# FFN up projection: 18 of 22 column pairs as seven products of half matrices, with the weights' sums formed by transfers

## The chip, the cores and the metric

The kernel runs on one core of a Trainium2 chip. The metric is the device time of one execution in microseconds, as the median of several executions. One core has TensorE (PE) for matrix products, VectorE (DVE), ScalarE (ACT) and GpSimd (POOL) for element-wise work, SyncE (SP) for issuing transfers, and 16 DMA engines that move data between DRAM and the on-chip memory SBUF. Matrix products land in PSUM, which has eight banks.

## The reference

One inference layer of a decoder (width 1024) is applied to 512 prompt tokens and 64 sample tokens, 576 in all. A mixer of three branches (gated linear attention, pooling, windowed attention) is followed by a gated feed-forward network (FFN) with a causal convolution of width 3; a norm of the result follows. The change lies in the FFN's first half:

```
def conv_ffn(xn, conv_prev, w_up, conv_w, conv_b, w_down):
    a, b = jnp.split(xn @ w_up, 2, axis=-1)          # xn: 576 x 1024, w_up: 1024 x 5632
    ext = jnp.concatenate([conv_prev.astype(a.dtype), a], axis=1)
    y = conv_b + conv_w[0] * ext[:, 0:t_len] + conv_w[1] * ext[:, 1:t_len + 1] + conv_w[2] * ext[:, 2:t_len + 2]
    h = jax.nn.silu(y) * b
    return h @ w_down, ext[:, -(CONV_WIDTH - 1):]    # w_down: 2816 x 1024
```

All data are float32. The output also holds the updated caches: 48 copies of cache rows, 120 to 2040 KB each, go from DRAM to DRAM.

## The kernel before

Every float32 product is made of three faster ones. Each operand is cut into hi, a rounded copy in the type F32R, and lo, the rest; the product is hi x hi + hi x lo + lo x hi, summed in PSUM. The activations lie with features on partitions, as eight tiles of 128 x 576 (`xh2`, `xl2` for the FFN). The weights come as a stream of chunks of 1024 rows x 128 columns (512 KB), in their order of use:

- `Chunk.load` (line 152) has SP issue the transfer into the tile `wr`, which has 3 buffers.
- `Chunk.split` cuts the whole chunk at once: ACT casts it into `wh` (line 161, 128x1024) and DVE subtracts for `wl` (line 164), 2 buffers each. For the first two chunks of the kernel POOL subtracts.
- `fetch(i)` cuts chunks i and i+1 and loads i+2 and i+3.
- `products` (matmul at line 207) runs over a chunk's eight k and the three terms; `gemm` does so for two parts of the tokens, each in one of the three PSUM banks `g`, and hands the bank to an evacuation.

The FFN's up projection is a loop over f = 0 to 21. A round takes a column pair: 128 columns of a and the 128 of b that they gate. So a round has 2 x 2 x 8 x 3 = 96 matmuls. The norm's factor per token, `rst`, is applied when the banks are read.

```
1164   for part, before in zip(SPLIT, (None, total)):
           gemm(P["a", f], XH2, XL2, evac, (part,))       # parts of 256 and 320 tokens; evac: DVE, lines 1159 and 1161
       ...                                                # two POOL copies into cc (1170, 1171), side_copy
1184   V.tensor_scalar(y, ae[:, 0:592], fvec[:, f, 16:17], fvec[:, f, 19:20], op0=OP.mult, op1=OP.add)
1185   V.scalar_tensor_tensor(y, ae[:, 1:593], fvec[:, f, 17:18], y, op0=OP.mult, op1=OP.add)
1186   V.scalar_tensor_tensor(y, ae[:, 2:594], fvec[:, f, 18:19], y, op0=OP.mult, op1=OP.add)
1187   S.activation(y, y, AF.Silu)
1189   G.tensor_tensor(yr[:, :NP], y[:, :NP], rst[:, :NP], op=OP.mult)     # and 1190 for the samples
       gemm(P["b", f], XH2, XL2, times(yr))               # DVE multiplies out of PSUM, line 226
1194   S.copy(h_hi[f], yr)
1195   V.tensor_tensor(h_lo[f], yr, h_hi[f].bitcast(F32), op=OP.subtract)
```

(Some calls above are shortened; the numbers at the left are the profile's lines.) `ae` holds a with the convolution's two earlier tokens, for the prompt and each of eight samples. `side_copy` (line 183) issues one of the DRAM copies on POOL's queue; there is one in each round.

The down projection (matmul at line 1249) follows: for each of eight blocks of 128 output columns, 22 k x 3 terms x 2 token halves, all of the block at once. `rows_out` turns a finished block to token rows. Block 7 is done in two token parts, so that the end is short.

The order of the work on each engine comes from a planner that knows the dependencies, the buffers and modelled durations of the instructions; `tc.issue_after` adds single constraints. Each engine runs its list in that order.

Of the kernel before, what the change touches and what calls it, by code (L numbers as in the profile page):

```python
# [22 lines left out]
NF = FF // 128  # L23
EPS = 1e-6
# [78 lines left out]
def hybrid_step(ctx: ExitStack, tc: tile.TileContext, I, O, at_a, at_b):  # L103
# [6 lines left out]
    xpool = ctx.enter_context(tc.tile_pool(name="x", bufs=1, side="left"))  # L110
# [25 lines left out]
    # ------------------------------------------------------- weight stream  # L136
    WSLOT = 1024
    chunks = []

    class Chunk:  # L140
        def __init__(self, src, kt, cols):
            self.src, self.kt, self.cols = src, kt, cols
            self.loaded = self.cut = False

        def load(self):
            if self.loaded:
                return
            self.loaded = True
            self.raw = wpool.tile([128, WSLOT], F32, tag="wr", name="wr", bufs=3)
            n = self.kt * self.cols  # L150
            self.v = self.raw[:, :n].rearrange("p (k c) -> p k c", k=self.kt)
            self.dma = nc.sync.dma_start(self.v, self.src)

        def split(self):
            if self.cut:
                return
            self.cut = True
            self.load()
            n = self.kt * self.cols
            hi = wpool.tile([128, WSLOT], F32R, tag="wh", name="wh", bufs=2)  # L160
            S.copy(hi[:, :n], self.raw[:, :n])  # L161
            lo = wpool.tile([128, WSLOT], F32R, tag="wl", name="wl", bufs=2)
            E = G if self in chunks[:2] else V
            self.cut_at = E.tensor_tensor(lo[:, :n], self.raw[:, :n], hi[:, :n].bitcast(F32), op=OP.subtract)  # L164
            self.hi = hi[:, :n].rearrange("p (k c) -> p k c", k=self.kt)
            self.lo = lo[:, :n].rearrange("p (k c) -> p k c", k=self.kt)
# [11 lines left out]
    def side_copy(after):  # L178
        """one of the copies within DRAM, issued behind an instruction of the Pool engine"""
        if copies:  # L180
            dst, src = copies.pop(0)
            with tc.issue_after(after.ins):
                nc.gpsimd.dma_start(dst, src)
# [5 lines left out]
    def plan(name, c0, cols=128, r0=0, kt=8):  # L189
        chunks.append(Chunk(rows(name, c0, cols, r0, kt), kt, cols))  # L190
        return len(chunks) - 1

    def fetch(i):
        for n in range(i, min(i + 2, len(chunks))):
            chunks[n].split()
        for n in range(i + 2, min(i + 4, len(chunks))):
            chunks[n].load()

    def products(ps, ids, xh, xl, t0, t1, c=0):
        """weights' hi and lo against the activations' hi and lo, into ps [128, t1 - t0]"""  # L200
        ks = [(i, k) for i in ids for k in range(chunks[i].kt)]
        for n, (i, k) in enumerate(ks):
            if k == 0:
                fetch(i)
            w = chunks[i]
            for j, (a, b) in enumerate(((w.hi, xh), (w.hi, xl), (w.lo, xh))):
                T.matmul(ps[:, :t1 - t0], a[:, k, c:c + 128], b(n)[:, t0:t1],  # L207
                         start=(n == 0 and j == 0), stop=(n == len(ks) - 1 and j == 2))
# [19 lines left out]
    def power(r, ms, e):  # L228
        """r = (ms + e) ** -0.5, two small tiles of one shape"""
# [3 lines left out]
    # ------------------------------------------------------------ constants  # L233
# [14 lines left out]
    # ------------------------------------------------------------ the plan of weight chunks, in order of use  # L248
# [45 lines left out]
    for f in range(NF):  # L294
        P["a", f] = [plan("ffn_w_up", 128 * f)]
        P["b", f] = [plan("ffn_w_up", FF + 128 * f)]
    for m in (*range(8), 7):
# [1000 lines left out]
```

## Time and profile before

| | |
|---|---|
| median of 3 runs | 1327.64 us (1325.46 to 1327.8) |
| span of the profiled execution, first to last instruction | 1324.9 us |
| PE busy | 1305.0 us, 99% |
| DVE busy | 601.6 us, 45% |
| ACT busy | 464.3 us, 35% |
| POOL busy | 242.4 us, 18% |
| mean rate of the DMA engines | 141 GB/s |
| up projection | 887.5 to 1171.3 us of the span |

The profiled execution has no time of its own other than the span; the runs' median lies 2.7 us above it. A busy time is the union of an engine's instructions; the matmuls' ends are modelled, so their number and pitch say more than their single durations. The DMA share is the time that packets took, as a share of 16 engines, and can pass 1 where packets overlap.

### The profile page before, as it was taken

Reading aid. Unit: us, or ns where it says so; the run is one execution under the profiler, and the core shown is the slowest. Engines: PE = TensorE matmul, PEld = TensorE weight load, DVE = VectorE, ACT = ScalarE, POOL = GpSimd, SP = SyncE. Lnnn points to the kernel's source line nnn. Section 1 sums busy time; section 2 is a strip of 40 time slices with the busy share of each in tenths; the row PEclk is TensorE's granted clock in tenths of the full one; section 3 lists DMA queues with packets and bytes.
Section 4 is the critical chain, followed back from the end, with each engine's and each line's share of the span. In section 5 each row is a group of like instructions: output and inputs, shape, how many; then the busy total and the mean of one; then the engine's idle time right before and its main releaser. Section 6 shows DMA issues by size and latency. Waiting matters only on the chain.

```text
span 1324.9 us, 23686 instructions
## 1 busy us (share of the span) xinstructions
PE 1305.0 (99%) x9903; PEld 1257.5 (95%) x9903; DVE 601.6 (45%) x1004; ACT 464.3 (35%) x899; POOL 242.4 (18%) x398
## 2 busy tenths in 40 slices
PE   8899999999999999999999999999999999999997
PEld 6899999999999999998988889999999999999997
DVE  5754564433453333162633366435555555532223
ACT  6554553534321222242433343433222222222223
POOL 4320211022410112041311110122121212200000
PEclk9999999999999999999999999999999999999999
DMA  7232432355443557266676415363455555444333
GB/s 218 65 116 68 144 115 69 96 178 158 131 141 95 163 159 220 73 184 190 182 217 204 154 31 167 100 225 118 145 164 162 162 167 157 148 129 149 91 88 116
DMA packets 220582, 187.44 MB, mean 141 GB/s; under 512 B 7900, under 2 KB 216393, under 8 KB 219700
## 3 DMA queue, kind: packets, MB, share of 16 engines
q1 hardware_dynamic: 218682, 142.28, 36.8%
q0 software_dynamic: 1792, 43.65, 9.6%
q8 instruction: 78, 1.28, 0.4%
q14 instruction: 28, 0.23, 0.1%
q10 hardware_dynamic: 2, 0.00, 0.0%
HBM read 175.52 MB, written 54.27 MB: 173 GB/s over the span
## 4 chain that ended last, share of the span: by engine, by line
PE 94%; DVE 2%; ACT 2%; issue 1%; DMA 1%; POOL 0%; SPq 0%; POOLq 0%; DVEq 0%; ACTq 0%
PE g L207 63%; PE g L1249 8%; PE g L395 8%; PE h L1249 2%; PE h L936 1%; PE s L805 1%; PE s L207 1%; PE s L864 1%; PE s L828 1%; PE s L820 1%; PE s L881 1%; PE h L869 1%; PE s L611 0%; DVE bb L475 0%; PE s L591 0%
## 5 line engine op out<-in xcount | busy, mean ns | idle before, releaser
L207 PE MATMUL g<-xl,wh 128*128 128x288 f32 (+2 forms) x1664 | 494.1, 297 | 0.0
L207 PE MATMUL g<-xh,wh 128*128 128x288 f32 (+2 forms) x1664 | 494.1, 297 | 0.0
L207 PE MATMUL g<-xh,wl 128*128 128x288 f32 (+2 forms) x1664 | 492.8, 297 | 1.1 <-DVE wl L164 1.1
L161 ACT CAST wh<-wr 128x1024 fp32r<-128x1024 f32 (+3 forms) x181 | 184.4, 1019 | 485.8 <-PE g L207 287.8
L164 DVE TENSOR_TENSOR wl<-wr,wh 128x1024 fp32r<-128x1024 f32 (+3 forms) x179 | 227.1, 1268 | 252.9 <-ACT wh L161 252.2
L207 PEld LDWEIGHTS g<-xh,wl 128*128 128x128 f32 x1664 | 313.7, 189 | 3.3 <-issue 1.4
L207 PEld LDWEIGHTS g<-xl,wh 128*128 128x128 f32 x1664 | 314.1, 189 | 2.3 <-issue 2.0
L207 PEld LDWEIGHTS g<-xh,wh 128*128 128x128 f32 x1664 | 314.2, 189 | 1.1 <-issue 0.7
L395 PE MATMUL g<-wh,xh 128*128 128x256 f32 x224 | 72.1, 323 | 2.5 <-DVE vs L400 2.5
L1249 PE MATMUL g<-hh,wl 128*128 128x288 f32 (+2 forms) x286 | 72.2, 297 | 0.0
L1249 PE MATMUL g<-hh,wh 128*128 128x288 f32 (+2 forms) x286 | 72.0, 297 | 0.0
L395 PE MATMUL g<-wl,xh 128*128 128x256 f32 x224 | 71.5, 319 | 0.0
L1249 PE MATMUL g<-hl,wh 128*128 128x288 f32 (+2 forms) x286 | 71.5, 295 | 0.0
L395 PE MATMUL g<-wh,xl 128*128 128x256 f32 x224 | 71.4, 320 | 0.0
L395 PEld LDWEIGHTS g<-wh,xh 128*128 128x128 f32 x224 | 52.3, 233 | 5.7 <-DVE vs L400 2.7
L395 PEld LDWEIGHTS g<-wl,xh 128*128 128x128 f32 x224 | 52.3, 234 | 0.7 <-issue 0.7
L395 PEld LDWEIGHTS g<-wh,xl 128*128 128x128 f32 x224 | 52.4, 234 | 0.0
L1249 PEld LDWEIGHTS g<-hh,wl 128*128 128x128 f32 x286 | 49.8, 189 | 0.0
L1249 PEld LDWEIGHTS g<-hh,wh 128*128 128x128 f32 x286 | 49.6, 189 | 0.0
L1249 PEld LDWEIGHTS g<-hl,wh 128*128 128x128 f32 x286 | 49.6, 189 | 0.0
L1159 DVE TENSOR_TENSOR ae<-g,rst 128x256 f32<-128x256 f32 x44 | 18.6, 425 | 64.0 <-PE g L207 64.0
L226 DVE TENSOR_TENSOR yr<-yr,g 128x288 f32<-128x288 f32 x44 | 18.1, 451 | 49.8 <-POOL yr L1189 49.8
(453 smaller groups left out, 2179.9 us busy)
## 6 DMA issues: line engine op xcount, KB each, us to landing
wr<-in_w_in_dram SPq DMA_DIRECT2D x74, 512.0 KB
wr<-in_ffn_w_up_dram SPq DMA_DIRECT2D x44, 512.0 KB
out_dram<-in_cache_k_w_dram POOLq DMA_DIRECT2D x8, 2040.0 KB, 8.4
out_dram<-in_cache_v_w_dram POOLq DMA_DIRECT2D x8, 2040.0 KB, 8.3
kv<-in_cache_k_w_dram SPq DMA_DIRECT2D x26, 512.0 KB
kv<-in_cache_v_w_dram SPq DMA_DIRECT2D x26, 512.0 KB
wr<-in_ffn_w_down_dram SPq DMA_DIRECT2D x18, 448.0 KB
wr<-in_ffn_w_down_dram SPq DMA_DIRECT2D x9, 512.0 KB
```

Source lines behind the costliest of these rows:

```text
L161: S.copy(hi[:, :n], self.raw[:, :n])
L164: self.cut_at = E.tensor_tensor(lo[:, :n], self.raw[:, :n], hi[:, :n].bitcast(F32), op=OP.subtract)
L207: T.matmul(ps[:, :t1 - t0], a[:, k, c:c + 128], b(n)[:, t0:t1], start=(n == 0 and j == 0), stop=(n == len(ks) - 1 and j == 2))
L226: return lambda ps, t0, t1: V.tensor_tensor(t[:, t0:t1], t[:, t0:t1], ps, op=OP.mult)
L395: mm = T.matmul(dst, a, b[:, n % 4, :], start=(n == 0 and j == 0), stop=(n == 7 and j == len(seq) - 1))
L805: T.matmul(sp[:, nk * n:nk * n + nk], qT[r, p, 128 * t:128 * t + 128], kT[r, p, k0:k0 + nk], start=True, stop=True)
L820: T.transpose(pt[:, 128 * n:128 * n + 128], s4[:, h, 128 * kb:128 * kb + 128], ident)
L828: T.matmul(po[64 * hh:64 * hh + 64, 128 * x:128 * x + 128], vt[:, blocks[kb], 64 * (2 * p + hh):64 * (2 * p + hh) + 64], pts[:, (2 * x + h ...
L864: T.transpose(pk[:, 128 * n:128 * n + 128], kt[:, 2 * half + n // 2, 128 * (n % 2):128 * (n % 2) + 128], ident)
L869: T.matmul(sp[32 * b:32 * b + 32, 0:128], qz[:, p, 32 * b:32 * b + 32], kT[:, n, p, :], start=(r == 0 and p == 0), stop=(r == NR[g] - 1 an ...
L1159: V.tensor_tensor(ae[:, 2 + t0:258 + t0], ps[:, :256], rst[:, t0:t0 + 256], op=OP.mult)
L1249: T.matmul(q[:, :t1 - t0], a[:, k, :], b[n][:, t0:t1], start=(n == 0 and j == 0), stop=(n == NF - 1 and j == 2))
```

## The change

**Seven products.** For f from 4 to 21 a pair is computed as a 2 x 2 block product. The activations are halved by features (k 0 to 3 and 4 to 7) and by tokens (two of 288); the weights of a pair are halved by rows (upper and lower 512) and by a or b. The Winograd form of Strassen's scheme makes the four result blocks from seven products of half matrices instead of eight. A product has 4 k x 3 terms = 12 matmuls of 288 columns. The rounds f = 0 to 3 stay as they were (`NF0 = 4`).

**x's parts.** `sums_x(k)`, called once after each of the first four rounds, forms the normed activations of k and k+4, four sums of their halves, and hi and lo of the seven parts: on DVE 13 operations, on ACT seven copies.

**Weights' sums.** The four summed operands t3, t2, t1, t4 are formed in place: a transfer with accumulation, issued by POOL, adds half a chunk (256 KB, in rows of 512 B) from DRAM to the half chunk in SBUF. t3, t2 and t4 are successive values of the same half of b's chunk. A part is cut (ACT and DVE, 512 columns) between its accumulation and the next. Loads, accumulations and cuts stand at set steps before the unit's first product (a step is a product).

**Sums of products.** Products 0, 2, 4, 6 accumulate in one bank A, 3 and 5 in B, 1 in C. Between two products of a bank ACT copies the bank's content (`s1`, `u2`, `s5`), or DVE adds it.

**The rest.** The cuts of all weights are made in pieces of 512 columns with 4 buffers instead of 1024 with 2. In the FFN's up projection the side copies are issued by ACT behind the SiLU instead of by POOL; the convolution's first step moves from DVE to ACT; h is kept in float32 and cut after the last pair, for all 22 f, in a pool that opens where x's parts were (every fourth lo on POOL, the others on DVE). Blocks m = 0 and 1 of the down projection run together, by thirds of the k and halves of a third. Comments were removed.

```diff
+        def piece(self, p):
+            if p not in self.parts:
+                self.load()
+                n = self.kt * self.cols
+                E = G if self in chunks[:2] else V
+                hi, lo, self.cut_at = cut_part(self.raw[:, PART * p:min(PART * p + PART, n)], E)
+                self.parts[p] = hi, lo
...
+    X_OF = ("11", "21", "t2", "t1", "t3", "22", "t4")
+    x_parts = {n: [sx.tile([128, 4, HALF], F32R, name=f"x{part}_{n}") for part in ("h", "l")] for n in X_OF}
+    def sums_x(k):
+        top = fp.tile([128, NT], F32, tag="xn", name="xn", bufs=1)
+        bottom = fp.tile([128, 592], F32, tag="y", name="xn2", bufs=1)[:, :NT]
+        for t, m in ((top, k), (bottom, k + 4)):
+            V.scalar_tensor_tensor(t, x1[:, m, :], vecs[:, m, 1:2], rst, op0=OP.mult, op1=OP.mult)
+        a11, a21, a12, a22 = top[:, :HALF], top[:, HALF:], bottom[:, :HALF], bottom[:, HALF:]
+        s3, s1, s2 = (fp.tile([128, HALF], F32, tag=t, name=t, bufs=2) for t in "uvu")
+        V.tensor_tensor(s3, a11, a21, op=OP.subtract)
+        V.tensor_tensor(s1, a22, a21, op=OP.subtract)
+        V.scalar_tensor_tensor(s2, s1, -1.0, a11, op0=OP.mult, op1=OP.subtract)
+        V.scalar_tensor_tensor(a21, a12, -1.0, s2, op0=OP.mult, op1=OP.subtract)
+        for n, x in (("11", a11), ("21", a12), ("t4", a22), ("t3", s3), ("t1", s1), ("t2", s2), ("22", a21)):
+            hi, lo = x_parts[n]
+            S.copy(hi[:, k], x)
+            V.tensor_tensor(lo[:, k], x, f32(hi[:, k]), op=OP.subtract)
+    class Unit:
+        def load(self):
+            self.b.load()
+            self.a.load(sx, "wr2", 2)
+        def place(self, n):
+            c, h = {"11": (self.a, 0), "t1": (self.a, 0), "21": (self.a, 4), "22": (self.b, 4)}.get(n, (self.b, 0))
+            return c.v[:, h:h + 4, :]
+        def add(self, n):
+            c, h = {"t3": (self.b, 4), "t2": (self.a, 0), "t4": (self.a, 4), "t1": (self.b, 0)}[n]
+            nc.gpsimd.dma_start(self.place(n), c.src[:, h:h + 4, :], accum_op=OP.add)
+        def cut(self, n):
+            pool, tag, bufs = {"t3": (sx, "3", 2), "t4": (sx, "4", 1)}.get(n, (wpool, "", 4))
+            src = self.place(n).rearrange("p k c -> p (k c)")
+            hi, lo = (pool.tile([128, PART], F32R, tag=f"w{t}{tag}", name=f"w{t}", bufs=bufs) for t in "hl")
+            S.copy(hi, src)
+            V.tensor_tensor(lo, src, f32(hi), op=OP.subtract)
+    ORDER = ("11", "21", "t2", "t1", "t3", "22", "t4")
+    STEPS_W = {-12: [("load", None)], -11: [("add", "t3")], -5: [("cut", "t3"), ("add", "t2")], -4: [("cut", "11"), ("add", "t1")],
+               -2: [("cut", "21")], -1: [("cut", "t2"), ("add", "t4")], 0: [("cut", "t1")], 1: [("cut", "22")], 4: [("cut", "t4")]}
...
+    for f in range(NF0, NF):
+        s1, u2, s5 = part("u"), part("v"), part("s5", 1)
+        A, B, C = big()[:, :HALF], small()[:, :HALF], small()[:, :HALF]
+        product(u, 0, A, True, False)
+        S.copy(s1, A)
+        product(u, 1, C, True, True)
+        V.tensor_tensor(ae[:, 2:2 + HALF], s1, C, op=OP.add)
+        product(u, 2, A, False, False)
+        S.copy(u2, A)
+        product(u, 3, B, True, False)
+        S.copy(s5, B)
+        product(u, 4, A, False, False)
+        V.tensor_tensor(h[:, HALF:], A, s5, op=OP.add)
+        product(u, 5, B, False, True)
+        V.tensor_tensor(h[:, :HALF], B, u2, op=OP.add)
+        product(u, 6, A, False, True)
+        n = NP - HALF
+        S.copy(ae[:, 2 + HALF:2 + NP], A[:, :n])
+        S.copy(aes[:, :, 2:10], by_sample(A[:, n:]))
+        keep_state(f, ae, aes)
+        y = conv(f, ae)
+        side_copy(y_at, nc.scalar)
+        V.scalar_tensor_tensor(h[:, :NP], h[:, :NP], -1.0, y[:, :NP], op0=OP.mult, op1=OP.mult)
+        V.scalar_tensor_tensor(by_sample(h[:, NP:]), by_sample(h[:, NP:]), -1.0, by_sample(y[:, 512:592])[:, :, 2:10],
+                               op0=OP.mult, op1=OP.mult)
...
+    for f in range(NF):
+        S.copy(h_hi[f], hs[f])
+        (G if f % 4 == 3 else V).tensor_tensor(h_lo[f], hs[f], f32(h_hi[f]), op=OP.subtract)
...
+    turns = [(m, chunks[P["dn", m][t]], p) for t in range(3) for p in range(2) for m in range(2)]
...
+    for x, (m, c, p) in enumerate(turns):
+        pieces(x)
...
+        for k in range(4 * p, min(4 * p + 4, c.kt)):
+            down_rows(c, k, n[m], ps[m], EVEN)
```

More of the change, by code (lines that the diff above doesn't have):

```diff
@@ L134, in close_pool, with cut_part, __init__, load @@
         cm.__exit__(None, None, None)
+    x_cm, xpool = open_pool("x", "left")
     WSLOT = 1024
+    PART = 512
     chunks = []
+    def cut_part(src, E):
+        n = src.shape[1]
+        hi = wpool.tile([128, PART], F32R, tag="wh", name="wh", bufs=4)
+        S.copy(hi[:, :n], src)
+        lo = wpool.tile([128, PART], F32R, tag="wl", name="wl", bufs=4)
+        return hi, lo, E.tensor_tensor(lo[:, :n], src, hi[:, :n].bitcast(F32), op=OP.subtract)
     class Chunk:
[L141 to L145, printed above, removed]
+        def __init__(self, src, kt, cols, plain=True):
+            self.src, self.kt, self.cols, self.plain = src, kt, cols, plain
+            self.loaded, self.parts = False, {}
+        def load(self, pool=None, tag="wr", bufs=3):
             if self.loaded:
@@ L152, in load, with at, wide @@
             self.dma = nc.sync.dma_start(self.v, self.src)
-        def split(self):
[L155 to L166, printed above, removed]
+        def piece(self, p):
[5 more added lines that the diff above has]
+                self.parts[p] = hi, lo
+            return self.parts[p]
+        def split(self):
+            if self.plain:
+                for p in range((self.kt * self.cols + PART - 1) // PART):
+                    self.piece(p)
+        def at(self, k, c=0):
+            a = k * self.cols + c
+            return [t[:, a % PART:a % PART + 128] for t in self.parts[a // PART]]
+        def wide(self, k):
+            a = k * self.cols
+            return [t[:, a % PART:a % PART + self.cols] for t in self.parts[a // PART]]
     KEYS = (("cache_k_w128", "cache_v_w128"), ("cache_k_w512", "cache_v_w512"), ("cache_k_w2048", "cache_v_w2048"))
@@ new lines, in hybrid_step, with pieces @@
+    units = [Unit(f) for f in range(NF0, NF)]
+    ORDER = ("11", "21", "t2", "t1", "t3", "22", "t4")
+    STEPS_W = {-12: [("load", None)], -11: [("add", "t3")], -5: [("cut", "t3"), ("add", "t2")], -4: [("cut", "11"), ("add", "t1")],
+               -2: [("cut", "21")], -1: [("cut", "t2"), ("add", "t4")], 0: [("cut", "t1")], 1: [("cut", "22")], 4: [("cut", "t4")]}
+    turns = [(m, chunks[P["dn", m][t]], p) for t in range(3) for p in range(2) for m in range(2)]
+    def pieces(n):
+        for _, c, p in turns[n:n + 4]:
+            c.piece(p)
+        for _, c, _ in turns[n + 4:n + 8]:
+            c.load()
@@ new lines, in steps, with product @@
+    def steps(g):
+        for at in sorted(STEPS_W, reverse=True):
+            u, r = divmod(g - at, 7)
+            if r == 0 and 0 <= u < len(units):
+                for what, n in STEPS_W[at]:
+                    getattr(units[u], what)(*([n] if n else []))
+        if g >= 7 * len(units) - 3:
+            pieces(0)
+    def product(u, p, ps, start, stop):
+        steps(7 * u + p)
+        n = ORDER[p]
+        (wh, wl), (xh, xl) = units[u].parts[n], x_parts[n]
+        for k in range(4):
+            for j, (a, b) in enumerate(((wh, xh), (wh, xl), (wl, xh))):
+                T.matmul(ps, a[:, 128 * k:128 * k + 128], b[:, k, :], start=start and k == 0 and j == 0,
+                         stop=k == 3 and j == 2, skip_group_check=True)
@@ L1156, in hybrid_step, with keep_state @@
         G.tensor_copy(aes[:, :, 0:2], fvec[:, f, 0:16].rearrange("p (b n) -> p b n", b=8))
-        def evac(ps, t0, t1):
-            V.tensor_tensor(ae[:, 2 + t0:258 + t0], ps[:, :256], rst[:, t0:t0 + 256], op=OP.mult)
-            if t0:
-                V.tensor_tensor(aes[:, :, 2:10], ps[:, 256:].rearrange("p (b n) -> p b n", b=8),
-                                rst[:, NP:].rearrange("p (b n) -> p b n", b=8), op=OP.mult)
-        for part, before in zip(SPLIT, (None, total)):
-            with tc.issue_after(before.ins) if f == 0 and before else nullcontext():
-                gemm(P["a", f], XH2, XL2, evac, (part,))
+        return ae, aes
+    def keep_state(f, ae, aes):
+        nonlocal cc
         i = f % 7
```

166 lines of the change are left out of this document (114 added, 52 removed).

## The prediction

> **What bounds the kernel now.** I read the page's totals first, then the chain that ended last in order of time, then the stretch of the FFN's up projection by itself.
>
> ```profile
> span 1324.9 us, 23686 instructions
> ...
> PE 1305.0 (99%) x9903; PEld 1257.5 (95%) x9903; DVE 601.6 (45%) x1004; ACT 464.3 (35%) x899; POOL 242.4 (18%) x398
> ...
> PE 94%; DVE 2%; ACT 2%; issue 1%; DMA 1%; POOL 0%; SPq 0%; POOLq 0%; DVEq 0%; ACTq 0%
> ```
> ```profile
> 896.87 80.03 PE g L207 x603
> 977.00 89.22 PE g L207 x672
> 1066.34 89.22 PE g L207 x672
> 1155.67 12.74 PE g L207 x96
> 1168.52 2.80 PE g L207 x21
> 1171.32 17.69 PE g L1249 x133
> ```
> ```profile
> 887.50:1171.30 283.80, 283.80 (x2144) 283.76 (x2145) 153.29 (x243) 77.48 (x97) 59.62 (x152) 1.00 0.51 154
> ```
>
> The first fence says that TensorE is busy nearly throughout and is 94% of the chain. The second says that the up projection is one unbroken run of matmuls at line 207: 672 of them take 89.22 us, so one costs 132.8 ns, a column pair (96) 12.745 us, and the next stage (line 1249) follows at once. The third is the same stretch as a window (time, PE, weight loads, DVE, ACT, POOL, clock, DMA share, GB/s): PE 283.80 of 283.80 at clock 1.00, DVE 54%, ACT 27%, DMA 0.51. So the number of matmuls sets the end here, and a matmul fewer is worth 0.1328 us, as long as nothing else becomes the bound.
>
> **The change part by part.** *Matmuls.* In 18 pairs, 96 matmuls become 7 products x 4 k x 3 = 84, all of 288 columns: 12 x 18 = 216 fewer, 216 x 0.1328 = -28.7 us. A unit (one pair) then lasts 84 x 0.1328 = 11.15 us and a product 1.593 us. The down projection's count is unchanged.
>
> *What must be done within 11.15 us.* The rows of this stretch by shape, for each engine:
>
> ```profile
> L164 DVE TENSOR_TENSOR wl<-wr,wh 128x1024 fp32r<-128x1024 f32 x43 | 52.6, 1222 | 13.3 <-ACT wh L161 13.1
> L1186 DVE SCALAR_TENSOR_TENSOR y<-ae,fvec,y 128x592 f32<-128x592 f32 x21 | 17.5, 835 | 0.7
> L226 DVE TENSOR_TENSOR yr<-yr,g 128x288 f32<-128x288 f32 x42 | 17.3, 452 | 47.5 <-POOL yr L1189 47.5
> L1195 DVE TENSOR_TENSOR hl<-yr,hh 128x576 fp32r<-128x576 f32 x20 | 15.0, 752 | 0.0
> L1184 DVE TENSOR_SCALAR y<-ae,fvec 128x592 f32<-128x592 f32 x21 | 12.4, 589 | 0.8
> L1161 DVE TENSOR_TENSOR ae<-g,rst 128x64 f32<-128x64 f32 x21 | 4.5, 215 | 0.0
> ```
> ```profile
> L161 ACT CAST wh<-wr 128x1024 fp32r<-128x1024 f32 x43 | 45.1, 1049 | 135.1 <-issue 85.5 <-PE g L207 49.6
> L1187 ACT ACTIVATE y<-y 128x592 f32<-128x592 f32 x21 | 14.7, 698 | 52.9 <-DVE y L1186 52.6
> L1194 ACT CAST hh<-yr 128x576 fp32r<-128x576 f32 x21 | 14.1, 671 | 1.3 <-DVE yr L226 1.3
> L1141 ACT COPY rst<-s 128x512 f32<-128x512 f32 x1 | 0.6, 590 | 0.1
> L1142 ACT COPY rst<-s 128x64 f32<-128x64 f32 x1 | 0.2, 205 | 0.0
> ```
> ```profile
> L152 SPq DMA_DIRECT2D wr<-in_ffn_w_up_dram x41: 367/368/452, 882.2 to 1141.6; - x41
> ```
>
> DVE: between 576 and 1024 elements a subtraction grows by (1222-752)/448 = 1.05 ns an element, so one of 512 is 0.685 us. Seven cuts 4.80, three sums out of PSUM at 0.452 make 1.36, two convolution steps 1.67, the last product 0.75 + 0.215: 8.8 us, 79%. ACT: a cast grows by 0.844 ns an element, 512 is 0.617; out of PSUM (590-205)/448 = 0.859, so 288 columns are 0.397 and 224 are 0.342. Seven cuts 4.32, three copies 1.19, the two of ae 0.55, Identity and SiLU at 0.698 make 1.40, and a side copy's issue, here at SP's 0.368: 7.8 us, 70%. Neither is the bound, but each is a queue in order.
>
> *Hand-offs.* Bank A takes products 0, 2, 4 and 6, bank B 3 and 5; ACT or DVE must read the bank in the one product between. The reader needs 0.397 to 0.452 us and may find one operation running (0.70 on ACT, 0.84 on DVE): 0.45 + 0.84 = 1.29, leaving 0.3 of 1.593 for the signals. One operation ahead costs nothing; two ahead cost PE about 0.4 us. The bounds are 0 and all four hand-offs late, 1.6 us a unit. I take 0.2 us a unit, one late in half the units: +4 us.
>
> *Sums of weights by transfers.* Each unit adds four accumulating transfers of 256 KB, issued by POOL, beside its two loads of 512 KB. No row shows an accumulating transfer. The rows nearest to it are the loads and the copies from 880 to 1160 us (queue: packets, MB, share of 16 engines; then KB each and us to landing):
>
> ```profile
> q1 hardware_dynamic: 44185, 22.15, 28.2%
> q0 software_dynamic: 816, 21.19, 22.2%
> ...
> out_dram<-in_cache_v_w_dram POOLq DMA_DIRECT2D x4, 2040.0 KB, 8.4
> ...
> out_dram<-in_cache_v_w_dram POOLq DMA_DIRECT2D x4, 504.0 KB, 3.9
> ...
> out_dram<-in_cache_v_w_dram POOLq DMA_DIRECT2D x4, 120.0 KB, 2.3
> ```
> ```profile
> 920.50:921.00 0.50, 0.50 (x5) 0.50 (x4) 0.00 (x0) 0.00 (x0) 0.00 (x0) 1.00 1.14 345
> ```
>
> Over these 280 us, q1's 22.15 MB are 42.3 loads of 0.524 MB and 79.0 us of engine time, 1.87 us a load; q0 is 62.2 us, 2.83 for each of 22 copies. The window is a lone load at its peak: share 1.14, 345 GB/s, which I take as full. If an accumulation costs what a load of its bytes does, a unit asks for 3.74 + 3.74 + 2.83 = 10.3 us of share, 10.3/1.14 = 9.0 us of 11.15: it fits. It reads two sources, the old sum and the new weights; if each read costs like a load, 3.74 + 7.48 + 2.83 = 14.05, over 1.14 is 12.3 us, and the transfers set the unit. Less than a load brings nothing, since PE is the bound then. I take something between 1 and 1.4 times: even 1.4 makes 3.74 + 5.24 + 2.83 = 11.8, 10.4 us, and costs nothing. The Trainium skill (Collectives: The Full Stack, section "The bandwidth ceiling: the fold count and why AG ≠ RS ≠ AR") speaks against this: it puts a reducing transfer at half the rate of a plain one since each chunk takes two reads. By that rule the sum would be the first rival's, below; no run here shows a reducing transfer.
>
> The chain t3, cut, t2, cut, t4 goes through one place in memory. From add t2 (step -5) to its product (step 2) are 7 steps, 11.15 us; less two cuts of 1.30 it has 8.5 us to land. By the landing rows 256 KB take about 3 us alone, but up to 3 + 8.4 behind a 2040 KB copy, late by 2.9 in about 6 of the 18 units (a third of the copies is that size). Bounds 0 and 18 us; I take +2, since the first load has the nearer row: it shared the engines with such copies throughout this stretch and PE waited for none.
>
> *POOL's queue.* The rows:
>
> ```profile
> L183 POOL DMA_DIRECT2D out_dram<-in_cache_v_w_dram x11 | 6.1, 556 | 0.4
> L1171 POOL COPY cc<-ae 128x16 f32<-128x16 f32 x21 | 4.1, 197 | 0.0
> L1170 POOL COPY cc<-ae 128x2 f32<-128x2 f32 x21 | 3.9, 185 | 140.8 <-DVE ae L1159 140.8
> L1156 POOL COPY ae<-fvec 128x16 f32<-128x16 f32 x20 | 3.9, 193 | 0.0
> L1155 POOL MEMSET ae<- 128x2 f32 x20 | 1.9, 93 | 52.2 <-DVE y L1186 52.2
> ```
>
> It keeps four small operations, 0.67 us a unit, loses the 1.28 us product of the other pairs and the side copies (now ACT's), and issues four accumulations. An issue is 0.556 us for a copy of 816/22 = 37 packets; an accumulation has 512 rows of 512 B. Bounds: 0.556, if the time is fixed, and 512/37 of it, 7.7 us, if it goes by the packet. POOL fills at (11.15-0.67)/4 = 2.62. I take 1.5, since copies of 120 and of 2040 KB were issued in the same 0.55: 6.7 us a unit, no cost. Behind add t3, which waits for its load, stand the unit's small POOL copies and t1 and t4; t4 has 7 steps to its product, so this wait is hidden unless the load is 5 us late.
>
> *Start of the units.* x's seven half matrices need, for each of four k, 13 DVE operations (two of 576 at about 0.82, eleven of 288 at about 0.43, 6.4 us) and seven copies on ACT. They need rst:
>
> ```profile
> L1159 DVE TENSOR_TENSOR ae<-g,rst x44: 415/425/427, 897.9 to 1164.9; 128x256 f32<-128x256 f32 x44
> ```
>
> Its first reader is at 897.9; the fourth pair ends at 1171.3 - 18 x 12.745 = 941.9. In these 44 us DVE has 4 x (6.9 of the window's 54%, less hl 0.75 and the step moved to ACT 0.59) = 22, sums 25.6, and four cuts 2.7, less some 4 done ahead: 46. It is over-full by 2 us, and the last sums queue behind the fourth pair's end: 0 to 7, I take +3.
>
> *Start of the down projection.* All 22 h are cut after the last unit. Tiles of hi lie where x's parts lay, so the first are free after that unit's product 0, but the lo of h2 and h3 lie on the part that its last product reads. PE needs 8 h in 12.75 us, ACT makes one in 0.671, DVE in 0.752 and POOL every fourth (a 512 there took 1.28): they keep ahead. Only the first lo can be late: 0 to 4, I take +1.
>
> *Elsewhere.* All other weights are cut in two pieces of 512, not one of 1024: DVE 2 x 0.685 - 1.222 = +0.15 us, ACT +0.19 a chunk, under PE with DVE at 45%. The first half is ready earlier, which can shorten waits. Both are hidden; bounds -2 and +2, taken as 0. Splitting m = 0 and 1 of the down projection by thirds moves no work to the tail, which still ends with m = 7.
>
> *Sum.* -28.7 + 4 + 2 + 3 + 1 = -18.7 us. The span is 1324.9 and the median of the runs 1327.6; the 2.7 us around the span stay: 1327.6 - 18.7 = 1309.
>
> **The rivals.** *First: the accumulations cost twice a load.* Then a unit is 12.33 us instead of 12.745, -7.5, plus 4 at the two ends: 1324. That is just inside faster; any further wait makes it the same. For it: two reads for each write. Against: at 0.51 the transfers are half idle now. This is the skill's rule.
>
> *Second, the other side: POOL's issue of 512 rows.* At t a piece a unit is 0.67 + 4t. It binds from 2.62, and from (12.52-0.67)/4 = 2.96 the kernel is slower than before. At 3.2 a unit is 13.5: 18 x 0.73 + 4 = +17, 1345. For it: no row has an issue of so many rows. Against: 0.55 at every size seen.
>
> *Third: late hand-offs.* DVE at 79% and ACT at 70% in order, SiLU waiting for DVE (the 52.6 us of its row) ahead of a bank's copy: 1 us a unit, -28.7 + 18 + 4 = -6.7, 1321. For it: PE has no slack between products of one bank. Against: DVE and ACT each still idle a fifth of the time.
>
> **How the numbers follow.** What tells from no change is 0.2%, 2.7 us: 1325.0 to 1330.3. The forecast, 1309 with a range of its own from 1299 (no stall at all) to 1317, gets 0.52; the first rival 0.17, the second 0.14, the third 0.15; 0.02 is left for orders that I have not seen. Faster: 0.52, most of the third (0.13) and under half of the first, which stands at the edge (0.07), 0.72. Slower: the second and a third of the first, 0.20. The rest, 0.08, is the same. The range 1299 to 1343 leaves out half of the second and a little below, some 0.1.
>
> **What would show it.** Right: 84 matmuls a unit in 11.2 to 11.5 us, POOL's accumulations under 2.6 us each, PE's idle time in the units under 8 us in all, a gap of some 3 us before the first unit. The first rival: DMA share near or over 1 in the units and ACT's cuts ended by DMA. The second: POOL busy without a gap. The third: PE's waits ended by ACT and DVE with the DMA share below 1. Wrong at the root: fewer than 216 matmuls gone, or other stages moved by over 2 us by the pieces of 512.

## The result, and the profile after

The changed kernel takes 1381.52 us (median of four runs, 1377.59 to 1382.7); the kernel before, run beside it, 1326.97 (1325.46 to 1327.8). The ratio is 1.0409, 95% interval 1.0393 to 1.0425: 4% slower, where 1.4% faster was forecast. The profiled execution has a span of 1379.8 us against 1324.9.

The page of the changed kernel, its span, totals, the slices of PE, of TensorE's clock and of DMA, and the queues:

```profile
span 1379.8 us, 24298 instructions
...
PE 1301.7 (94%) x9687; PEld 1246.0 (90%) x9687; DVE 668.3 (48%) x1258; ACT 576.6 (42%) x1270; POOL 315.6 (23%) x419
...
PE   8999999999999999999999999997897887969997
...
PEclk9999999999999999999999999999999998989999
DMA  7232333453444454556675135747999999835323
...
q0 software_dynamic: 38992, 42.92, 16.0%
```

The matmuls did go: 9903 became 9687, 216 fewer. But PE, 99% busy before, is 94% busy, and most of its new idle time lies in the slices in which the DMA row reads 9 (the slice with a 6 holds the passage to the down projection). A window over most of the units (960 to 1140 us: time, PE, weight loads, DVE, ACT, POOL, clock, DMA share, GB/s), of the changed kernel and of the one before:

```profile
960.00:1140.00 180.00, 154.49 (x1064) 150.14 (x1062) 97.70 (x172) 84.23 (x177) 76.06 (x97) 0.94 1.02 203
```
```profile
960.00:1140.00 180.00, 180.00 (x1358) 180.00 (x1357) 98.46 (x157) 48.55 (x59) 37.51 (x100) 1.00 0.52 158
```

The DMA share went from 0.52 to 1.02. DVE is no busier than before and ACT is under half, so neither is full. But 1.02 is a mean, and no even load. Two stretches within this window:

```profile
1001.00:1008.00 7.00, 7.00 (x54) 6.81 (x52) 2.92 (x6) 2.74 (x6) 0.56 (x4) 1.00 1.29 201
1008.75:1009.50 0.75, 0.00 (x0) 0.00 (x0) 0.04 (x1) 0.00 (x0) 0.75 (x1) 1.00 0.00 0
```

For 7 us the share was 1.29 and PE had work; soon after, for 0.75 us, the DMA engines moved nothing while PE stood and POOL was issuing the next transfer. In half-microseconds, about half of the window's 180 us lie above 1.15 and over a fifth below 0.5. So the engines are crowded for much of the time, but not full all the time. PE lost time twice: 180 - 154.5 = 25.5 us idle, and its 1064 matmuls, at 0.1328 us, are 141.3 us of work that took 154.5, so 13.2 us went to a lower granted clock (0.94). The queues in the same window (packets, MB, share of 16 engines; then issues with KB each and median us to landing):

```profile
q0 software_dynamic: 25542, 12.69, 56.9%
q1 hardware_dynamic: 25536, 12.75, 28.1%
q10 hardware_dynamic: 448, 10.91, 17.0%
...
wr<-in_ffn_w_up_dram POOLq DMA_DIRECT2D x49, 256.0 KB, 6.8
```

q0 is now the accumulating transfers alone: 12.69 MB are 48.4 of 0.262 MB, and 0.569 x 180 = 102.4 us of the engines, 2.12 us each. q1, the weight loads, moved as many bytes for half of that. Who waited, in the same window:

```profile
ACT wh L1227 <- DMA wr<-in_ffn_w_up_dram: 60.5, 24, 7.8
POOL wr L1221 <- DVE wl L1228: 51.0, 21, 9.9
POOL wr L1221 <- DMA wr<-in_ffn_w_up_dram: 22.3, 6, 12.0
```

ACT's cuts wait for transfers, POOL's next transfers wait for those cuts or for a load, and PE waits for ACT. The units run from the first of these matmuls to the last (line 1263; min/median/max ns, first and last start):

```profile
L1263 PE MATMUL g<-xh,wh x72: 293/298/442, 947.6 to 1193.0; 128*128 128x288 f32 x72
...
L1263 PE MATMUL g<-xh_t,wl x216: 289/295/606, 958.2 to 1210.4; 128*128 128x288 f32 x108
```

That is (1210.4 - 947.6)/18 = 14.6 us a unit, where 11.15 was the work and 12.745 a pair before. In what follows, "a unit" is always this quotient.

**The terms.** The prediction's sum, less the 2.7 us around the span, was 1306.2; the span is 1379.8. Of the difference of 73.6, 2.7 is the start (first unit at 947.6, not 944.9), 56.1 the units (262.8 us, not 206.7), 9.8 the passage to the down projection (10.8 us, not 1) and 5.0 what follows (158.6 us, not 153.6). The units and the passage are the two things to explain.

### The profile page after: what moved, and what is told of

Same layout as the page of the kernel before. It is cut to its first block, busy times and chain, and to the rows that moved or that the text cites. A ratio compares the mean times of both kernels' runs of the same rounds, so it can differ in the third digit from the quotient of the medians.

```text
span 1379.8 us, 24298 instructions
## 1 busy us (share of the span) xinstructions
PE 1301.7 (94%) x9687; PEld 1246.0 (90%) x9687; DVE 668.3 (48%) x1258; ACT 576.6 (42%) x1270; POOL 315.6 (23%) x419
## 5 line engine op out<-in xcount | busy, mean ns | idle before, releaser
L149 DVE TENSOR_TENSOR wl<-wr,wh 128x512 fp32r<-128x512 f32 (+2 forms) x282 | 200.1, 711 | 321.7 <-ACT wh L147 315.4
L230 PE MATMUL g<-xh,wh 128*128 128x288 f32 (+2 forms) x1088 | 325.5, 299 | 4.4 <-DVE h L249 2.7
L230 PE MATMUL g<-xh,wl 128*128 128x288 f32 (+2 forms) x1088 | 325.0, 299 | 0.0
L230 PE MATMUL g<-xl,wh 128*128 128x288 f32 (+2 forms) x1088 | 324.0, 298 | 0.0
L147 ACT CAST wh<-wr 128x512 fp32r<-128x512 f32 (+2 forms) x286 | 173.2, 608 | 335.2 <-PE g L230 224.3
L230 PEld LDWEIGHTS g<-xh,wh 128*128 128x128 f32 x1088 | 206.2, 190 | 7.9 <-DVE h L249 3.1
L230 PEld LDWEIGHTS g<-xl,wh 128*128 128x128 f32 x1088 | 206.0, 189 | 1.4 <-issue 1.1
L230 PEld LDWEIGHTS g<-xh,wl 128*128 128x128 f32 x1088 | 206.2, 190 | 1.0 <-issue 0.6
L1228 DVE TENSOR_TENSOR wl<-wr,wh 128x512 fp32r<-128x512 f32 x126 | 85.4, 689 | 101.9 <-ACT wh L1227 97.7
L1221 POOL DMA_DIRECT2D wr<-in_ffn_w_up_dram x72 | 95.1, 1485 | 141.6 <-DVE wl L1228 82.7
```

The costliest lines, as they stand in the source:

```text
L147: S.copy(hi[:, :n], src)
L149: return hi, lo, E.tensor_tensor(lo[:, :n], src, hi[:, :n].bitcast(F32), op=OP.subtract)
L230: T.matmul(ps[:, :t1 - t0], a, b(n)[:, t0:t1], start=(n == 0 and j == 0), stop=(n == len(ks) - 1 and j == 2))
L1221: nc.gpsimd.dma_start(self.place(n), c.src[:, h:h + 4, :], accum_op=OP.add)
L1228: V.tensor_tensor(lo, src, f32(hi), op=OP.subtract)
```

## The experiments

The theories: **throughput** (the DMA engines set the pace, since an accumulating transfer takes 2.1 us of them: 4 x 2.12 + 3.74 + 2.83 = 15.0 us a unit, and over the 1.02 of the window 14.7; since 2.12 and 1.02 come from this same window, that this meets 14.6 is bookkeeping and proves nothing yet), **order** (transfers land late behind large copies, and the queues of ACT and POOL, each in order, pass the delay on) and **hand-offs** (ACT and DVE, whatever the transfers do). The four runs of the changed kernel lie within 5.1 us, so a single run is good to some 5 us.

**1. No side copies in the units.**

```diff
-        side_copy(y_at, nc.scalar)
+        del copies[:1]
```

> Left out: the side copies that would be issued in the eighteen units (one 2040 KB copy a unit; the rows they would bring stay unwritten). Throughput theory (an accumulating transfer takes some 2.1 us of the sixteen DMA engines, so a unit needs 8.4 + 3.7 + 2.8 = 15.0 us of them and gets 14.7): without the 2.8 us a unit needs 12.1 us, so 18 units save 18 x 2.6 = 47 us: 1333 us, with the DMA share still at 1 in the units. Latency theory (an accumulating transfer is late only when it queues behind a copy of 2040 KB, and ACT's queue, which is in order, then holds the bank copies): with the copies gone it lands in some 3 us, ACT never waits, a unit takes 11.2 to 11.5 us: 1318 to 1323 us. Hand-off theory (PE waits for the cuts and bank copies on ACT and DVE whatever the DMA does): a unit stays at 14 us or more, 1370 us or more.

1356.8 us, 13.24 a unit, DMA share 0.93. It lies between: not at the 12.1 us of throughput, nor near the 11.2 to 11.5 of order. The 53 transfers of the window still landed after 6.1 us at the median (6.8 with the copies), so the copies were not the main thing that made them late.

**2. The four transfers as plain loads.**

```diff
-            nc.gpsimd.dma_start(self.place(n), c.src[:, h:h + 4, :], accum_op=OP.add)
+            nc.gpsimd.dma_start(self.place(n), c.src[:, h:h + 4, :])
```

> The four accumulating transfers of a unit become plain loads of the same 256 KB into the same place, issued by POOL at the same points: the sums are not formed. Throughput and latency theories, which both put the loss on the accumulation: the four transfers cost 4 x 0.94 = 3.8 us of the engines instead of 8.4, the unit needs 10.3 us of them, less than PE's 11.15, and takes 11.2 to 11.8 us: 18 x 3 us less than 1380, so 1318 to 1330 us. If POOL's issue of the transfers is what is late, or the hand-offs of ACT and DVE, nothing changes: 1375 us or more.

1328.6 us, 11.72 a unit. The same window, and its queue of POOL's transfers:

```profile
960.00:1140.00 180.00, 178.50 (x1345) 177.80 (x1344) 125.18 (x219) 107.45 (x221) 60.60 (x123) 1.00 0.86 260
```
```profile
q0 software_dynamic: 5029, 16.50, 31.5%
...
wr<-in_ffn_w_up_dram POOLq DMA_DIRECT2D x63, 256.0 KB, 4.6
```

16.50 MB are 62.9 transfers in 56.7 us, 0.90 us each: the same bytes, issued by the same engine at the same steps, cost 2.12 when they accumulate, 2.35 times as much. 53 of the 65 us that this and the next run recover hang on the word "accumulate". The hand-off theory falls. POOL's issue also became shorter, 0.747 us at the median for 1.286, but POOL was busy 76 of 180 us in the changed kernel's window, so its issue was not what filled a unit.

**3. No transfers at all.** The line of the four transfers is deleted.

> The four accumulating transfers of a unit are left out altogether: the cuts are made from the weights as loaded, the sums are not formed. What is left of the loss is that of the hand-offs on ACT and DVE and of the passage to the down projection. If these cost what the forecast said (0.2 us a unit), a unit takes 11.3 us, 1315 us with the 10 us passage kept. Hand-off theory: a unit stays over 12 us, 1330 us or more. If this run and the one with plain loads agree within 4 us, the bytes of the added transfers cost nothing and only their accumulation does.

1316.5 us, 11.24 a unit: in the window PE is busy 180.00 of 180 us at clock 1.00. The hand-offs inside the units cost 0.1 us each unit. The run with plain loads is 12 us above this one, so their bytes are not quite free at a share of 0.86.

**4. Two cst tiles.**

```diff
-            cst_o = fp.tile([126, 128], F32, tag="cst", name="cst", bufs=1)
+            cst_o = fp.tile([126, 128], F32, tag="cst", name="cst", bufs=2)
```

> The tile that holds the convolution states before they are written out (cst) has two buffers instead of one; all else is as in the changed kernel. In the trace ACT waited 5.6 us at the end of the units for the last writes out of that tile, with the casts of the activations queued behind it, and PE stood some 10 us. If that wait holds the chain, the gap at the passage shrinks to 3 to 5 us and the time falls by 5 to 7 us: 1373 to 1376 us. If the backlog of ACT or DVE holds it, the copy is no longer waited for but the gap stays near 10 us: 1379 us or more.

1380.2 us; no gain that a single run can tell. PE's gap shrank from 10.8 to 7.1 us only. ACT's stretch at the passage, in the changed kernel and in this one (start, us, operation, idle time before it and its releaser):

```profile
1213.98 0.70 ACT L1274 ACTIVATE y<-y 128x592 f32<-128x592 f32 x1 [1.77 <-DVE y L1272]
1215.84 0.52 ACTq L205 DMA_DIRECT2D out_dram<-in_cache_k_w_dram  x1
1220.32 0.26 ACT L1297 COPY cst<-s 18x128 f32<-18x128 f32 x1 [5.64 <-DMA out_dram<-cst]
1220.48 3.54 ACT L1375 CAST hh<-h 128x576 fp32r<-128x576 f32 x6
```
```profile
1210.86 0.24 ACT L1297 COPY cst<-s 18x128 f32<-18x128 f32 x1
1212.73 0.70 ACT L1274 ACTIVATE y<-y 128x592 f32<-128x592 f32 x1 [1.63 <-DVE y L1272]
1214.91 0.52 ACTq L205 DMA_DIRECT2D out_dram<-in_cache_k_w_dram  x1
1215.52 3.54 ACT L1375 CAST hh<-h 128x576 fp32r<-128x576 f32 x6 [2.10 <-DMA out_dram<-cst]
```

The copy no longer waits, but the first casts now do, for the same writes: the tiles of hh take the memory in which cst lay. The convolution ahead of the casts is the rest of the gap.

**5. The sums on POOL.** Line 1221's transfer is replaced by an operation in SBUF (t1 as t2 less the lower half of b's load, since b's upper half is overwritten by then):

```diff
+            old = self.b.v[:, 0:4, :] if n == "t1" else self.place(n)
+            G.tensor_tensor(self.place(n), old, c.v[:, h:h + 4, :], op=OP.subtract if n == "t1" else OP.add)
```

> The four sums of a unit are formed by POOL in SBUF (128x512 additions and one subtraction) in place of the accumulating transfers; all else as in the changed kernel. A 128x512 product of two tiles took POOL 1.31 us elsewhere in these traces, so a unit gives POOL 4 x 1.3 = 5.3 us of work beside 11.15 us of PE. Throughput theory: the DMA engines are freed of 8.4 us a unit and the loss goes, as in the run without additions: 1316 to 1322 us. Hand-off theory, or a POOL that slows DVE beside it: 1335 us or more, with DVE's cuts longer than in the run without additions.

1327.4 us, between the two expectations, 11.58 a unit, share 0.53: the engines are freed and most of the loss goes. What stays over the run without sums I put down to DVE (no run tests this by itself; in run 12 DVE hardly got lighter). Its cut, and POOL's sum, in the window; first the run without sums, then this one:

```profile
L1227 DVE TENSOR_TENSOR wl<-wr,wh 128x512 fp32r<-128x512 f32 x111 | 76.4, 689 | 28.9 <-ACT wh L1226 24.8 <-PE g L1262 1.9 <-PE s L1262 0.4
...
L1363 DVE SCALAR_TENSOR_TENSOR h<-h,y 128x512 f32<-128x512 f32 x16 | 11.0, 687 | 1.6 <-ACT y L1273 1.6
```
```profile
L1229 DVE TENSOR_TENSOR wl<-wr,wh 128x512 fp32r<-128x512 f32 x110 | 101.1, 940 | 3.1 <-ACT wh L1228 3.0
...
L1365 DVE SCALAR_TENSOR_TENSOR h<-h,y 128x512 f32<-128x512 f32 x15 | 21.2, 1414 | 0.0
```
```profile
L1222 POOL TENSOR_TENSOR wr<-wr 128x512 f32<-128x512 f32 x63 | 95.6, 1525 | 55.4 <-DVE wl L1229 45.0 <-DMA wr<-in_ffn_w_up_dram 3.6 <-DVE y L1273 2.7
```

Beside POOL's 1.5 us sums DVE's cut goes from 0.689 to 0.940 us and its product from 0.687 to 1.414, and DVE is full (177.4 of 180 us). The Trainium skill (GPSIMD Engine Reference, section "8. Key points") says that the two engines share SBUF interfaces and contend when DVE has two SBUF inputs; these rows agree, and DVE's sums that read PSUM kept their time (0.453 and 0.445 us).

**6. Half the sums on POOL** (t1 and t4; t3 and t2 by transfers).

> Only the second and fourth of the four sums (t1 and t4) are formed by POOL; t3 and t2 stay accumulating transfers. Throughput theory: a unit needs 2 x 2.1 + 3.7 + 2.8 = 10.7 us of the engines, less than PE's 11.15, so nearly all of the loss goes though two transfers stay: a unit takes 11.2 to 12 us, 1318 to 1332 us. Latency theory: t3 and t2 are the first of the chain and still land in 6 us or more behind the copies with ACT's queue waiting at their cuts, so most of the loss stays: 1345 us or more.

1364.5 us, 13.62 a unit at a share of 0.76. By its expectation this speaks for order, and I took the throughput theory for open again. But the run changed two things: t1's subtraction stands in POOL's queue until t2's transfer has landed. POOL in one unit:

```profile
1073.69 1.30 POOL L1225 DMA_DIRECT2D wr<-in_ffn_w_up_dram  x1 [1.50 <-DVE h L1360]
...
1082.90 1.29 POOL L1223 TENSOR_TENSOR wr<-wr 128x512 f32<-128x512 f32 x1 [6.51 <-issue]
```

After that transfer and two small copies POOL stood 6.5 us; ACT's cut of what the transfer brought began at 1082.80, POOL's subtraction at 1082.90. Then the next transfer and the fourth sum went, all late. So the run cannot tell the two in the changed kernel, but it shows the cost of order here: at a share of 0.76 the engines were not full.

**7. The passage alone.** The last unit's convolution is issued behind the first four casts, and its tiles (ae, y, cst) lie where no cast comes:

```diff
     for f in range(NF):
+        if f == 4:
+            finish_unit()
         S.copy(h_hi[f], hs[f])
```

> The accumulating transfers stay; only the passage to the down projection is changed. The last unit's convolution is issued behind the first four casts of the activations (on ACT, DVE and POOL), and the tiles it uses (its ae and y, the states' cst) lie where the casts do not come, so that no cast waits for a write of states to land. If the 10 us gap of PE at the passage comes from the casts' wait for those writes and for the convolution ahead of them, the gap shrinks to 2 to 4 us: 1372 to 1375 us. If DVE's and ACT's backlog sets it, 1379 us or more.

1363.4 us, 18 below the changed kernel. PE's gap is 1.5 us, even less than the 2 to 4 expected; but that is 9.3 of the 18. The units also ran in 13.97 us, not 14.6, some 11 us in all, and PE now waits 5.0 us later on, for a weight's remainder. The edit also changed the order in which the planner puts instructions outside the passage, and I did not trace the 11 us to one of those changes; they stay open. But they bear on the theories. From the first unit's first matmul to the last one's, in the changed kernel and here:

```profile
947.60:1210.40 262.80, 223.76 (x1516) 216.38 (x1515) 150.24 (x268) 125.14 (x260) 108.52 (x140) 0.93 0.99 196
```
```profile
948.40:1199.90 251.50, 221.39 (x1516) 215.26 (x1515) 149.53 (x265) 123.56 (x258) 106.11 (x138) 0.93 1.01 204
```

The same matmuls and nearly the same transfers took 11 us less. The accumulating transfers, loads and copies were all still there, so something besides their engine time, most likely the order of the work, had a part in what the changed kernel lost.

**8. Sums on POOL and the new passage.** The edits of 5 and 7.

> Both together: the sums on POOL and the new passage. If the two losses are separate, the gains add: the run with the sums on POOL less 6 to 8 us, 1309 to 1316 us, some 0.7 to 1.3 per cent faster than the kernel before. If the units' loss hides the passage's, less.

1318.95 us (1318.15 to 1319.62); ratio to before 0.994, 0.9924 to 0.9957: 0.6% below the kernel before, clear of the noise though small, and 4.5% below the changed kernel. Against the run with sums on POOL the passage brought 8.4 us (that run is a single one). The gains add, but the sum misses the expected 1309 to 1316, since run 5 came out above its 1316 to 1322.

**9. Half on POOL, no copies.** The edits of 6 and 1.

> As the run with half the sums on POOL (1364.5 us, 13.6 us a unit, DMA share 0.80), and the eighteen side copies of the units left out (their rows stay unwritten). That run needed only 4.2 + 3.7 + 2.8 = 10.7 us of the engines a unit, so a full DMA cannot be what held it. If its t3 and t2 waited behind the 2040 KB copies: a unit falls to about what it takes with all sums on POOL, 11.6 to 12 us, 1328 to 1336 us. If the two transfers' own time from issue to landing (4.9 us there) holds the chain through POOL's and ACT's queues, copies or not: 13 us or more, 1350 us or more.

1343.7 us, 12.79 a unit, at a share of 0.64: between the two expectations. Here neither the engines nor DVE (141 of 180 us) is full, and still 1.2 us a unit are lost against all sums on POOL. With these two sums of each kind the order does cost.

**10. t2 one product earlier**, all four by transfers.

```diff
-    -5: [("cut", "t3"), ("add", "t2")]
+    -6: [("cut", "t3"), ("add", "t2")]
```

> All four sums by accumulating transfers, copies in; t3 is cut and the t2 transfer issued one product (1.6 us) earlier. Throughput theory (15 us of the engines a unit): the same 14.4 to 14.6 us a unit, 1376 to 1384 us. Order theory (ACT's wait at the cut of t2 is what PE loses): up to 1.6 us a unit less, 1352 to 1368 us.

1383.5 us, 14.53 a unit, share 1.00: no change, though the transfer was asked for 1.6 us earlier. As throughput says; order is refuted in the form that it has here, t2's late landing alone. Run 7's shorter units speak against refuting every order.

**11. Casts interleaved with the down products** (on top of 8; in the source, a few casts ahead of each turn in place of all 22 before the first).

> Sums on POOL and the new passage, and the casts of the activations are issued a few ahead of the down products that use them, not all 22 before the first. In the run with sums on POOL and the new passage PE lost some 7 us at 1171 to 1180 us, where the fifth weight piece's remainder stood behind seventeen casts on DVE. With that gone: 1311 to 1314 us (from 1319). If another wait takes its place: 1316 us or more.

1318.63 us (ratio 0.9936, 0.992 to 0.9953): as 8. The wait of 5.0 us is still there, and ACT still made fifteen casts in one run: the planner had kept the order, so the idea was not tested.

**12. t3 by a transfer, three sums on POOL** (on top of 11).

> As the interleaved one, but the first sum of a unit (t3), which has six products of time, is formed by an accumulating transfer and three by POOL. DVE was busy 40.0 of 40 us beside POOL's four sums; with three it gets back about a quarter of what they cost it (its cut took 0.94 us beside them and 0.69 without). A unit then falls from 11.58 towards 11.3 us: 3 to 5 us below the interleaved one. If the transfer's landing (behind a 2040 KB copy) holds POOL's queue, with the next sums behind it, it is slower than the interleaved one, by 5 us or more.

1320.85 us (ratio 0.9956, 0.9941 to 0.9971), 11.64 a unit against 11.57. DVE was still busy 174.6 of 180 us (176.5 in run 11), so hardly any of its time came back.

**13 and 14. Two accumulate, two are plain**, every transfer issued where it was: no operation on POOL, the same engine time in both.

```diff
-c.src[:, h:h + 4, :], accum_op=OP.add)
+c.src[:, h:h + 4, :], **({"accum_op": OP.add} if n in ("t3", "t1") else {}))
```

> Of a unit's four transfers by POOL, t3 and t1 accumulate and t2 and t4 are plain loads of the same bytes (their sums are not formed). Engine time a unit: 2 x 2.1 + 2 x 0.9 + 3.74 + 2.83 = 12.6 us. Throughput theory: 12.2 to 12.8 us a unit, halfway between the run with four plain loads (11.72) and the changed kernel (14.6): 1336 to 1350 us, and the same, within 6 us, as the run in which the other two accumulate. Order theory (the cuts of t2 and t4, which come soonest after their issue, block ACT): near the run with four plain loads, 1328 to 1334 us.

> The mirror: t2 and t4 accumulate, t3 and t1 are plain loads (their sums are not formed). Throughput theory: 12.2 to 12.8 us a unit, 1336 to 1350 us, within 6 us of the mirror. Order theory: most of the loss stays, 13.5 us a unit or more, 1360 us or more.

1359.2 and 1355.3 us; 13.35 and 13.08 a unit. Their windows:

```profile
960.00:1140.00 180.00, 162.86 (x1163) 158.48 (x1163) 107.67 (x191) 92.01 (x193) 69.87 (x108) 0.97 0.93 221
```
```profile
960.00:1140.00 180.00, 164.42 (x1187) 160.41 (x1185) 109.56 (x194) 93.95 (x198) 71.10 (x110) 0.98 0.94 227
```

Within 4 us of each other, and halfway between none accumulating (11.72) and all four (14.6), which is 13.16. Which pair it is, the early or the late one of the chain, makes no difference that single runs can tell; how many accumulate does. That refutes order as I had put it, which asked for 1328 to 1334 us from one and 1360 or more from its mirror. Throughput missed too: 12.2 to 12.8 us a unit took the engines at a share of 1.0, and they were at 0.93 and 0.94. A unit of 13.1 to 13.4 us at such a share says that something else than full engines also takes time.

**What the runs show together.** That the transfers accumulate is worth 53 us (run 2). The loss grows with their number and not with their place (13, 14). How a transfer's price turns into time is only in part shown: by engine time (2.12 us for 0.90), by later landing, and by queues in order that leave the engines idle for a time (the share of 0.00 above; runs 1 and 9 lay between the two theories, and run 6 lost 2 us a unit against run 5 at a share of 0.76). No run separates these in the changed kernel.

**15. Casts held back by order marks** (on top of 11).

> The interleaved version (sums on POOL, new passage), with the casts of the activations from the seventh on, and the last unit's convolution, held back by an order mark behind the down products of the turn before, so that the planner cannot pull them ahead. In the interleaved run DVE and ACT still did all casts first and PE waited 5.0 us for a weight's remainder, then ran at a granted clock of 0.55 to 0.6 for some 5 us. With that gone: 1311 to 1314 us. If the marks only move the wait: 1317 us or more.

1318.65 us (ratio 0.9938, 0.9924 to 0.9951). ACT's order at the passage was again fifteen casts in a row and the wait 4.8 us; the marks did not do what I wanted, and the run says nothing about the wait's cause.

**16. Every second remainder of the activations on POOL** (on top of 8).

```diff
-        (G if f % 4 == 3 else V).tensor_tensor(h_lo[f], hs[f], f32(h_hi[f]), op=OP.subtract)
+        (G if f % 2 else V).tensor_tensor(h_lo[f], hs[f], f32(h_hi[f]), op=OP.subtract)
```

> As the run with the sums on POOL and the new passage (1319 us), but every second, not every fourth, remainder of the activations (hl) is formed by POOL. DVE's seventeen of 0.7 to 1.0 us become eleven, some 5 us less ahead of the weights' remainders that PE waited 5.0 us for. If DVE's backlog is that wait: it goes, and with it the half-speed TensorE behind it: 1312 to 1315 us. If POOL (1.5 to 1.9 us each, and slowing DVE) is then late instead: 1318 us or more.

1321.84 us (ratio 0.9965, 0.9953 to 0.9976), worse than 8; the wait, which DVE ends, grew to 7.6 us. POOL's line:

```profile
L1387 POOL TENSOR_TENSOR hl<-h,hh 128x576 fp32r<-128x576 f32 x11 | 20.1, 1864 | 6.1 <-ACT hh L1386 6.1
```

At 1.86 us each POOL's eleven take 20.1 us. Beside them DVE's eleven took 1.61 us each, where DVE's seventeen took 1.10 in run 8: 17.1 us against 17.7, so the smaller number brought nothing. What would take this wait away is open.

## Why the prediction was wrong

*Matmuls*: right. 216 went, and where nothing else bound (run 3) a unit took 11.24 us against 11.15.

*Sums of weights by transfers*: this is the step that failed. "I take something between 1 and 1.4 times" was a choice between two bounds, 1 and 2, with no row of an accumulating transfer, and it went to the side of the nearest row, a plain load; so a term that "costs nothing" stood in the sum. The price is 2.35 times, outside the bounds, and it cost most of the 56 us that the units took too long: with plain transfers in the same places 53 us came back (run 2). No rival reached the result either; the slowest had 1345. The Trainium skill's rule that I set beside it (Collectives: The Full Stack, "The bandwidth ceiling: the fold count and why AG ≠ RS ≠ AR": stated there for collectives: a reducing transfer at half rate, for its two reads) had the right direction, and 2.35 goes a little beyond its 2.

A second error in the same step: I divided by 1.14, the share of one lone load in half a microsecond, as if the engines could be kept at it through a whole unit. As a peak 1.14 was not even high (1.29 for 7 us, above); but the mean over 180 us was only 0.93 to 1.04 in the seven kernels with two or four accumulating transfers a unit and no sum on POOL, with gaps in between. At a mean of 1.02 even 1.4 times would have made 11.6 us, already over PE's 11.15: the step had no room for its own upper choice.

*The first rival* was therefore the right mechanism, with its marks as written (a share over 1 in the units, ACT's cuts ended by DMA), as far as the transfers' price goes, but it too was sized by 1.14 and by two reads: 12.3 us a unit and 1324, not 14.6 and 1382. It had no term for the gaps. It also left out the clock: after PE has stood for some microseconds, it comes back slow. In the changed kernel, PE after one such wait (start, us, operation):

```profile
1053.45 0.40 PE L1263 MATMUL g<-xh_t,wh 128*128 128x288 f32 x1 [3.53 <-ACT wh L1227]
...
1056.02 0.44 PE L1263 MATMUL g<-xh_t,wh 128*128 128x288 f32 x1
1056.26 0.44 PE L1263 MATMUL g<-xl_t,wh 128*128 128x288 f32 x1
...
1057.48 0.30 PE L1263 MATMUL s<-xl_t,wh 128*128 128x288 f32 x1
1057.61 0.30 PE L1263 MATMUL s<-xh_t,wl 128*128 128x288 f32 x1
```

Starts 0.24 us apart, then 0.13: for some 3.5 us after a wait of 3.5 the matmuls ran at about half pace. The Trainium skill (TensorE: Matmul & The Clock Gate, "What's actually happening") puts the default clock at half and says that an idle window of about 3.4 us brings it back; this row agrees. By PE's account a third of what the units lost in the window stands under the lower clock, 13.2 of 38.7 us. That is not shown to be time that a full clock would have saved: where PE then waits for a transfer anyway, faster matmuls only lengthen the wait.

*The chain t3, t2, t4* (+2): "256 KB take about 3 us alone" was read from copies; an accumulating one took 6.1 us with no copies beside it and 6.8 with them. More time for t2 (run 10) bought nothing, so this wait alone was not the term. Runs 6 and 9 show that, at shares of 0.76 and 0.64, the order can cost 1 to 2 us a unit, and run 7's units were 0.6 shorter with all four transfers.

*Hand-offs* (+4): 0.1 us a unit in run 3; too high if anything. The third rival falls. *POOL's queue*: taken as 1.5 us, measured

```profile
L1221 POOL DMA_DIRECT2D wr<-in_ffn_w_up_dram x72 | 95.1, 1485 | 141.6 <-DVE wl L1228 82.7
```

so the second rival falls; POOL waited longer (141.6 us) than it issued (95.1). *Start of the units* (+3): 5.7, inside 0 to 7, but by luck. The term was priced as DVE over-full with x's sums. In the changed kernel DVE stood for 8.07 us in that stretch, behind a cut on ACT that waited for a transfer:

```profile
942.47 0.62 ACT L1227 CAST wh<-wr 128x512 fp32r<-128x512 f32 x1 [10.44 <-DMA wr<-in_ffn_w_up_dram]
```

Without the four transfers (run 3), with the same sums on DVE, the first unit began at 942.7, 0.8 us behind the 941.9 of the prediction; with plain ones (run 2) at 945.9. So these microseconds were the transfers', not DVE's. *Elsewhere* (0): that same 0.8 leaves no room for over 2 us before the units.

*Start of the down projection* (+1, bounds 0 to 4): 10.8 us. I looked at which memory x's parts leave and not at the convolution of the last unit, whose writes of states and whose chain through ACT and DVE now come after the last matmul; before, the second half of the last pair's matmuls covered them. Runs 4 and 7 show both. The 5.0 us after it are a wait of 2.9 for a weight's remainder on DVE, and PE's slow restart: 64 matmuls in the first 10 us, where the kernel before had 78, are some 1.9 us.

## What to carry to other kernels

Price an accumulating transfer from a run of one before building on it: here it took 2.35 times the engine time of a plain load of the same bytes, and moving sums "into the transfers" turned a kernel bound by PE into one that waits for transfers. Do not set the engine time of a unit against the peak of a lone load: the mean share here stayed near 1 though a stretch of 7 us reached 1.29, since in other stretches the engines had little to do. And look at what the last unit's matmuls used to cover: here the last unit's convolution, in ACT's and DVE's order ahead of the casts, stood bare at the passage for 10.8 us.

## What was not expected of the hardware

- An accumulating transfer of 256 KB from DRAM into SBUF: 2.12 us of the sixteen engines, 4.5 us to land at least and 6.5 at the median in the changed kernel; a plain one by the same queue 0.90 us, 3.3 at least and 4.5.
- The accumulating ones moved in packets of 497 bytes on average (12.69 MB in 25542), the plain ones by the same queue in packets of 3281 (16.50 MB in 5029). Short packets are not the price by themselves: SP's loads ran in 499-byte packets and took 1.04 us for 256 KB (28.1% of 180 us for 12.75 MB).
- POOL's sums of two SBUF tiles cost DVE nearly as much as the same work on DVE would have: four sums a unit raised DVE from 131.6 to 177.4 us in 180, 45.8 us over 63 sums, 0.73 us each, where a 128x512 subtraction on DVE alone is 0.689.
